# Gated embedding added by transfers, and a ninth pair by seven products, in the last stage of a Hymba block

## The chip, the cores and the metric

The kernel runs on one core of a Trainium2 chip. The metric is the device time of one execution in microseconds (us), taken as the median of several runs. A core has TensorE (PE in the profile, with PEld for its weight loads), VectorE (DVE), ScalarE (ACT), GpSimd (POOL) and SyncE (SP), which run side by side and wait for each other on semaphores, and 16 DMA engines. DMAs are put on queues by SP, by ACT and by POOL.

## The reference

One layer of a block over 256 positions and 4096 columns. Its last part, which the change is in:

```python
h = h + jnp.concatenate([y_a, y_c], axis=-1) @ w_out[i]
gate = jax.nn.sigmoid(rms_norm(h, ple_norm_g[i]) @ w_ple_gate[i] + b_ple_gate[i])
h = h + gate * (p[i] @ w_ple[i])
return rms_norm(h, final_g)
```

`w_ple_gate` is 4096 x 4096, `w_ple` is 256 x 4096; all is float32.

## The kernel before

A matrix product of 256 positions by 4096 rows of weights is made for two blocks of 512 columns at a time. That is a *group*; the last stage has four, and `c0` = 0, 2, 4, 6 is the first of each group's two blocks. I call them groups 1 to 4. The rows are walked in 16 *pairs* of two blocks of 128. `product` and `mixed_product` load a pair's weights (`wt`) with SP and split each into a rounded high part `wh`, cast by ACT (L204), and a low part `wl` = `wt` - `wh`, made by DVE (L205). Each product is made three times (high by high, low by high, high by low).

A *plain* pair takes 2 x 2 x 2 x 3 = 24 products of TensorE. A pair *by seven* uses Strassen's scheme in Winograd's form: 7 x 3 = 21, for which DVE sums weights into `ua` and `ub` (L518, L519, L531, L532), and these are split too, into `uh` and `ul`. It also needs combined left sides, which `combined_parts` makes ahead. For pair 13 there is no tile for them; `combine_into_places(13, ...)` puts them into free corners of the first four operand tiles, once for each left operand.

The string of pairs (`dense`, `denser`, `late`, `final`) is the order of a group. `*` is a pair by seven; `-` means that the low part of its second block is made by a transfer: ACT writes the negated high part into `low` (L217), and a DMA on POOL's queue adds the weights to it (L495, L524).

`later` is a queue of small work of the group before. `fill` takes four of its entries after each pair (`fills=(4,)`). In the last stage these are, for each of the four quarters (256 positions in two halves `h`, two blocks `j`): the gate times the embedding (`z`), the sum of that and the residual `hc`, the sum of squares of `hc` (ACT, L610) and `hc` times the last weight `fgs`. All but the squares are by DVE, and the profile has them at L184. The group's own end is the product of the embedding (`product(w_ple[0], ...)`, 24 products at L237).

The program gives the order in which the work is written; a scheduler then sets each engine's order by its own estimates of durations. Each engine takes its instructions in that order. Only what is in `pin` keeps the order in which it is written. Buffers of one `tag` go round: `wh` and `wl` have three each, `uh` and `ul` two.

Of the kernel before, what the change touches and what calls it, by code (L numbers as in the profile page):

```python
# [13 lines left out]
ALU = mybir.AluOpType  # L14
# [11 lines left out]
def hybrid_block(  # L26
# [23 lines left out]
    nc = tc.nc  # L50
# [129 lines left out]
    later = deque()  # L180
# [62 lines left out]
    def product(w, col, lhs, kblocks, pool=None, tag="acc", fills=2):  # L243

        acc = [
            (pool or ps_acc).tile([P, NB], F32, tag=tag, name=f"acc{h}") for h in range(NH)
        ]
        for k0 in range(0, kblocks, KC):
            kc = min(KC, kblocks - k0)
            wh, wl = weight_parts(w, col, k0, kc)  # L250
            for k in range(kc):
                for h in range(NH):
                    accumulate(acc[h], h, lhs, k0 + k, wh, wl, k, kblocks)
            fill(fills)
        return acc
# [10 lines left out]
    def sum_rows():  # L266
        return [spool.tile([P, NB], F32, tag="row", name="comb", bufs=3) for _ in range(2)]
# [33 lines left out]
    def combine_again(dst, at, t, i, rows, then=lambda ins: None, at_places=None):  # L301

        a, s = rows
        then(
            nc.vector.tensor_tensor(
                a.rearrange("q (i t) -> q i t", t=T), t[:, i : i + 2, 0, :].bitcast(F32),
                t[:, i : i + 2, 1, :].bitcast(F32), ALU.add,
            )
        )
        return combined_parts(  # L310
            dst, at, s, a[:, :T], a[:, T : T + P], a[:, T + P :], 1.0, then, at_places
        )
# [27 lines left out]
    def units(text):  # L340

        return [
            (int(u.rstrip("*+-")), "".join(f for f in "*+" if f in u), "-" in u)
            for u in text.split()
        ]


    dense = units("1 0* 3 2* 5 4* 6* 7 8* 9 10* 11 12* 14* 13 15")
    denser = units("1 0* 3 2* 5 4* 13* 7- 6*- 8* 10*- 9 12* 14* 11 15")
# [12 lines left out]
    late = units("1 3 5 7 9 11 13 15 0* 2 4* 6 8* 10* 12 14")  # L362

    def spare_places(tiles):

        return [[t[:, 0, q, P:] for q in range(2)] for t in tiles]
# [3 lines left out]
    def combine_into_places(pair, tiles):  # L370

        rows = sum_rows()
        places[pair] = spare_places(tiles[:4])
        t, i = tiles[pair // 2], pair % 2 * 2
        combine_again(None, None, t, i, rows, at_places=places[pair])()
# [193 lines left out]
    tt, stt = nc.vector.tensor_tensor, nc.vector.scalar_tensor_tensor  # L569
    QUARTERS = ((0, 0), (1, 0), (0, 1), (1, 1))  # L570

    def helper_sums(helper, z):


        nc.scalar.copy(z[1][0], helper["P1"])
        tt(z[1][0], helper["P6"], z[1][0], ALU.add)
        tt(z[0][1], helper["P5"], z[1][0], ALU.add)
        tt(z[1][0], helper["P7"], z[1][0], ALU.add)
        tt(z[1][1], helper["P5"], z[1][0], ALU.add)

    def sum_tiles(*homes):

        homes = homes or (dict(tag="stage"),) * 2
        t = [spool.tile([P, NH, NB], F32, name="z", **kw) for kw in homes]
        return t, [[t[j][:, h] for j in range(2)] for h in range(NH)]
# [481 lines left out]
    def broadcast_row(src, n0, n, **kw):  # L1067

        kw = kw or dict(tag="row", bufs=3)
        t = spool.tile([P, n], F32, name="row", **kw)  # L1070
        nc.sync.dma_start(
            t, bass.AP(tensor=src.tensor, offset=src.offset + n0, ap=[[0, P], [1, n]])
        )
        return t
# [101 lines left out]
    hs, hT, hS = [], [], []  # L1176
# [20 lines left out]
    for c0 in range(0, D // NB, 2):  # L1197
        for j in range(2):
            hc = act.tile([P, NH, NB], F32, tag="act", name="hc")
# [20 lines left out]
        for h, j in QUARTERS:  # L1220
            hc = hs[c0 + j][:, h, :]
# [10 lines left out]
    ssq_f = cpool.tile([P, NH, n_f + 2], F32, name="ssq_f")  # L1232
    nc.vector.memset(ssq_f[:, :, :1], EPS)
    square_f = partial(square_sum, scale=D ** -0.5)

    def gated_pair(c0, order, ahead):

        z, rows, fgs = [], [], []

        def on_begin():  # L1240
            rows.extend(broadcast_row(b_ple_gate, (c0 + j) * NB, NB) for j in range(2))

        def on_helpers(helper):
            z.extend(sum_tiles()[1])
            stt(z[0][0], helper["P1"], r_h[:, :1], rows[0], ALU.mult, ALU.add)
            helper_sums(helper, z)
            for h, j in QUARTERS[1:]:
                zz = z[h][j]
                stt(
                    zz, zz, r_h[:, h : h + 1], rows[j],  # L1250
                    ALU.mult, ALU.subtract if j else ALU.add,
                )
            fgs.extend(broadcast_row(final_g, (c0 + j) * NB, NB) for j in range(2))

        acc = mixed_product(
            w_ple_gate[0], c0 * NB, hT, hS, order, on_helpers, ahead=ahead, fills=(4,),
            on_begin=on_begin,
        )
        pacc = [
            product(w_ple[0], (c0 + j) * NB, pT, PLE // P, pool=ps_tmp, tag="tmp", fills=0)  # L1260
            for j in range(2)
        ]
        todo = []
        for h, j in QUARTERS:
            gt, hc = z[h][j], hs[c0 + j][:, h, :]
            stt(gt, acc[h][j], r_h[:, h : h + 1], gt, ALU.mult, ALU.subtract if j else ALU.add)
            nc.scalar.activation(gt, gt, AF.Sigmoid)
            later.append(partial(tt, gt, pacc[j][h], gt, ALU.mult))
            todo.append(partial(tt, hc, hc, gt, ALU.add))
            todo.append(partial(square_f, ssq_f[:, h, 1 + c0 + j : 2 + c0 + j], hc))  # L1270
            todo.append(partial(tt, hc, hc, fgs[j], ALU.mult))
        later.extend(todo)

    for c0 in range(0, n_f - 2, 2):
        gated_pair(c0, dense if c0 else late, None if c0 else h_ahead)


    c0 = n_f - 2
# [9 lines left out]
    rows, fgs = [], []  # L1288
# [90 lines left out]
    squares = []  # L1379
# [45 lines left out]
```

## Time and profile before

| | us |
|---|---|
| median of the runs | 2024.87 |
| lowest run | 2024.77 |
| profiled execution | 2025.85 |
| its span (first to last instruction) | 2024.1 |
| PE busy in it | 2006.7 |
| DVE busy | 1926.9 |
| ACT busy | 1257.1 |
| POOL busy | 65.3 |

Busy time counts stretches in which at least one instruction of an engine runs; matmuls overlap, and their ends are modelled, so a busy PE is not proof of PE at its peak. Start times are us from the span's start. In the chain of waits each row is what the end of the span was waiting for at that moment. In groups of instructions the first number after the bar is the busy time, the second the mean of one in ns, then the idle time of the engine just before and what ended it. The time "to landing" runs from a DMA's issue to the update of its semaphore.

### The profile page before, as it was taken

To read this page: it belongs to the slowest core of one execution; us is meant where nothing else is said; L and a number is where in the kernel's file an instruction comes from. 1 tells how busy PE (TensorE), PEld (TensorE's weight loads), DVE (VectorE), ACT (ScalarE), POOL (GpSimd) and SP (SyncE) were. 2 spreads that over 40 slices of the span, in tenths; PEclk is the share of its full clock that TensorE was granted. 3 is DMA by queue.
4 is the path that set the end of the run, shared out by engine and by line. 5 is a ranking of instruction groups with operands and counts; after the bars stand their busy time and mean duration, and the time that the engine had idled before them with its cause. 6 is when DMAs were issued, how large, how long until landed. Compare 5 with 4: busy or idle time off the path is not lost.

```text
span 2024.1 us, 26329 instructions
## 1 busy us (share of the span) xinstructions
PE 2006.7 (99%) x9043; PEld 1648.0 (81%) x9043; DVE 1926.9 (95%) x2771; ACT 1257.1 (62%) x1634; POOL 65.3 (3%) x71
## 2 busy tenths in 40 slices
PE   9999999999999999999999999999999999999997
PEld 7888888878888888788888888887888888888876
DVE  7999999899999999888999999999999999999998
ACT  7655555665666556776566676765766766656565
POOL 0000000000000000000000000000000000000000
PEclk9999999999999999999999999999999999999999
DMA  8788878679668877556677786876767766666765
GB/s 290 225 233 241 249 221 250 178 220 257 200 198 257 255 206 235 164 176 205 202 239 215 225 244 209 240 239 204 236 215 230 234 200 200 211 218 206 232 207 180
DMA packets 174193, 447.72 MB, mean 221 GB/s; under 512 B 14302, under 2 KB 17518, under 8 KB 174058
## 3 DMA queue, kind: packets, MB, share of 16 engines
q1 hardware_dynamic: 161952, 417.93, 63.8%
q0 software_dynamic: 11456, 27.27, 7.9%
q8 instruction: 71, 1.16, 0.2%
q10 hardware_dynamic: 650, 0.84, 0.1%
q14 instruction: 64, 0.52, 0.1%
HBM read 441.78 MB, written 4.19 MB: 220 GB/s over the span
## 4 chain that ended last, share of the span: by engine, by line
PE 89%; DVE 6%; issue 2%; DMA 1%; ACT 1%; POOLq 0%; POOL 0%; ACTq 0%; DVEq 0%; SPq 0%
PE acc L420 68%; PE acc_P L420 17%; DVE wl L205 2%; DMA wt<-in_w_in_dram 1%; PE tmp_ps L170 1%; DVE cv L787 1%; PE acc L237 1%; DVE ul L205 1%; PE tmp_ps L959 0%; PE tmp_ps L943 0%; PE tmp_ps L977 0%; ACT uh L204 0%; DVE cv L868 0%; ACT wh L204 0%; PE tmp_ps L982 0%
## 5 line engine op out<-in xcount | busy, mean ns | idle before, releaser
L420 PE MATMUL acc<-wh,big_t 128*128 128x512 f32 x4028 | 1240.3, 391 | 0.9 <-ACT big_t L156 0.4
L204 ACT CAST wh<-wt 128x1024 fp32r<-128x1024 f32 (+1 forms) x716 | 684.3, 965 | 493.8 <-PE acc L420 351.7
L420 PEld LDWEIGHTS acc<-wh,big_t 128*128 128x128 f32 x4028 | 753.3, 188 | 157.1 <-issue 1.3
L205 DVE TENSOR_TENSOR wl<-wt,wh 128x1024 fp32r<-128x1024 f32 (+1 forms) x716 | 788.8, 1113 | 33.0 <-ACT wh L204 27.5
L420 PE MATMUL acc<-wl,big_t 128*128 128x512 f32 x1958 | 756.4, 392 | 0.3 <-DVE wl L205 0.2
L420 PEld LDWEIGHTS acc<-wl,big_t 128*128 128x128 f32 x1958 | 367.2, 188 | 78.1 <-DVE wl L205 2.7
L204 ACT CAST uh<-ua 128x1024 fp32r<-128x1024 f32 x187 | 196.6, 1051 | 103.0 <-DVE ua L519 51.7
L205 DVE TENSOR_TENSOR ul<-ua,uh 128x1024 fp32r<-128x1024 f32 x187 | 228.1, 1220 | 6.9 <-ACT uh L204 4.2
L787 DVE SCALAR_TENSOR_TENSOR cv<-uT,dw,cv 128x255 f32<-128x255 f32 (+23 forms) x480 | 203.6, 463 | 1.1
L420 PE MATMUL acc_P<-uh,big_t 128*128 128x512 f32 x570 | 174.6, 391 | 0.1
L204 ACT CAST uh<-ub 128x1024 fp32r<-128x1024 f32 x99 | 104.2, 1053 | 47.9 <-DVE ub L532 39.2
L420 PEld LDWEIGHTS acc_P<-uh,big_t 128*128 128x128 f32 x570 | 106.0, 188 | 24.5 <-ACT uh L204 3.3
L205 DVE TENSOR_TENSOR ul<-ub,uh 128x1024 fp32r<-128x1024 f32 x99 | 120.8, 1220 | 0.8 <-ACT uh L204 0.5
L420 PE MATMUL acc_P<-ul,big_t 128*128 128x512 f32 x285 | 109.7, 392 | 0.2 <-DVE ul L205 0.2
L420 PE MATMUL acc<-uh,big_t 128*128 128x512 f32 x286 | 88.6, 390 | 0.0
L420 PE MATMUL acc_P<-wh,big_t 128*128 128x512 f32 x286 | 88.3, 389 | 0.0
L518 DVE TENSOR_TENSOR ua<-wt 128x512 f32<-128x512 f32 x112 | 76.9, 686 | 10.0 <-DMA wt<-in_w_in_dram 6.2
L519 DVE TENSOR_TENSOR ua<-wt 128x512 f32<-128x512 f32 x112 | 76.8, 686 | 2.7 <-DMA wt<-in_w_in_dram 1.7
L420 PE MATMUL acc_P<-uh,comb_t 128*128 128x512 f32 x228 | 70.3, 391 | 0.3 <-ACT uh L204 0.2
L532 DVE TENSOR_TENSOR ub<-ub,wt 128x512 f32<-128x512 f32 x99 | 68.1, 688 | 1.4
L531 DVE TENSOR_TENSOR ub<-ua,wt 128x512 f32<-128x512 f32 x99 | 67.8, 685 | 0.0
L420 PEld LDWEIGHTS acc_P<-ul,big_t 128*128 128x128 f32 x285 | 53.3, 188 | 13.9 <-DVE ul L205 3.0
(254 smaller groups left out, 1631.0 us busy)
## 6 DMA issues: line engine op xcount, KB each, us to landing
wt<-in_w_in_dram SPq DMA_DIRECT2D x416, 512.0 KB, 4.7
wt<-in_w_out_dram SPq DMA_DIRECT2D x128, 512.0 KB, 4.5
wt<-in_w_ple_gate_dram SPq DMA_DIRECT2D x128, 512.0 KB, 4.2
wt<-in_w_pw_dram SPq DMA_DIRECT2D x32, 512.0 KB, 4.9
ua<-in_w_in_dram SPq DMA_DIRECT2D x31, 512.0 KB, 4.3
ua<-in_w_in_dram POOLq DMA_DIRECT2D x31, 512.0 KB, 8.8
wt<-in_w_in_dram SPq DMA_DIRECT2D x31, 256.0 KB, 2.8
low<-in_w_in_dram POOLq DMA_DIRECT2D x12, 512.0 KB, 8.2
```

Of the source, the lines that this page charges most:

```text
L170: nc.tensor.transpose(pt[:, i * T + h * P : i * T + (h + 1) * P], src[:, h, b] if len(src.shape) == 4 else src[:, h, b * P : (b + 1) * P], ...
L204: nc.scalar.copy(wh[:, :kc, :], wt[:, :kc, :]),
L205: nc.vector.tensor_tensor(wl[:, :kc, :], wt[:, :kc, :], wh[:, :kc, :].bitcast(F32), ALU.subtract),
L237: nc.tensor.matmul(acc, a, b[:, k, :], start=kb == 0 and kind == 0, stop=kb == kblocks - 1 and kind == 2,)
L420: nc.tensor.matmul(banks[name], a, b, start=name not in begun, stop=final and ends[name] == n and kind == 2 and not (left and name in "P2 ...
L518: plus(ua[:, 0], w0[:, 0], w0[:, 1])
L519: plus(ua[:, 1], w0[:, 1], w1[:, 1])
L531: plus(ub[:, 0], ua[:, 0], w1[:, 1])
L532: plus(ub[:, 1], ub[:, 0], w1[:, 0])
L787: nc.vector.scalar_tensor_tensor(cv[:, i, PAD - k :], uT[:, i, : T + k - PAD], dw[:, b, k : k + 1], cv[:, i, PAD - k :], ALU.mult, ALU.add,)
```

## The change

It has three parts.

- The sum of gated embedding and residual (`tt(hc, hc, gt, ALU.add)` on DVE, twelve in all) becomes a DMA on POOL's queue that adds `gt` to `hc`. It is written right behind the product that makes `gt`. Squares and weighted copies are written after all four of them, squares first.
- Groups 2 and 3 use `denser` in place of `dense`: nine pairs by seven in place of eight, and three low parts by transfers in place of none.
- `combine_into_places(13, hT)` is called once, after group 1.

```diff
-        todo = []
+        squares, weights = [], []
         for h, j in QUARTERS:
             gt, hc = z[h][j], hs[c0 + j][:, h, :]
             stt(gt, acc[h][j], r_h[:, h : h + 1], gt, ALU.mult, ALU.subtract if j else ALU.add)
             nc.scalar.activation(gt, gt, AF.Sigmoid)
             later.append(partial(tt, gt, pacc[j][h], gt, ALU.mult))
-            todo.append(partial(tt, hc, hc, gt, ALU.add))
-            todo.append(partial(square_f, ssq_f[:, h, 1 + c0 + j : 2 + c0 + j], hc))
-            todo.append(partial(tt, hc, hc, fgs[j], ALU.mult))
-        later.extend(todo)
+            later.append(partial(nc.gpsimd.dma_start, hc, gt, accum_op=ALU.add))
+            squares.append(partial(square_f, ssq_f[:, h, 1 + c0 + j : 2 + c0 + j], hc))
+            weights.append(partial(tt, hc, hc, fgs[j], ALU.mult))
+        later.extend(squares + weights)
 
     for c0 in range(0, n_f - 2, 2):
-        gated_pair(c0, dense if c0 else late, None if c0 else h_ahead)
+        gated_pair(c0, denser if c0 else late, None if c0 else h_ahead)
+        if c0 == 0:
+            combine_into_places(13, hT)
```

The two orders and the functions that the new call uses (unchanged):

```python
    dense = units("1 0* 3 2* 5 4* 6* 7 8* 9 10* 11 12* 14* 13 15")
    denser = units("1 0* 3 2* 5 4* 13* 7- 6*- 8* 10*- 9 12* 14* 11 15")
...
    def combine_into_places(pair, tiles):

        rows = sum_rows()
        places[pair] = spare_places(tiles[:4])
        t, i = tiles[pair // 2], pair % 2 * 2
        combine_again(None, None, t, i, rows, at_places=places[pair])()
```

ACT's order at the start of group 2, before (`junk` with `ssq_f` is a square of `hc`; what stands in brackets are the semaphores waited for, DMASW those of POOL's DMAs, DMAHW those of SP's, DVE, PE and Activation those of the engines):

```order
L204 CAST uh<-ua 128x1024 [waits DVE_49]
L204 CAST wh<-wt 128x1024 [waits DMAHW4_49,PE_49,Activation_49]
L204 CAST wh<-wt 128x1024 [waits DMAHW5_49,DVE_49,PE_49]
L204 CAST wh<-wt 128x1024 [waits DMAHW6_49,DVE_49,PE_49]
L204 CAST uh<-ub 128x1024 [waits DVE_49]
L610 ACTIVATE junk,ssq_f<-hc 128x512
L204 CAST wh<-wt 128x512 [waits DMAHW7_49,PE_49,Activation_49]
L610 ACTIVATE junk,ssq_f<-hc 128x512 [waits DVE_49,Activation_49]
```

The same place now:

```order
L204 CAST uh<-ua 128x1024 [waits DVE_49]
L610 ACTIVATE junk,ssq_f<-hc 128x512 [waits DMASW4_49]
L610 ACTIVATE junk,ssq_f<-hc 128x512 [waits DMASW5_49,Activation_49]
L204 CAST wh<-wt 128x1024 [waits DMAHW3_49,PE_49]
L204 CAST uh<-ub 128x1024 [waits DVE_49]
L204 CAST wh<-wt 128x1024 [waits DMAHW4_49,PE_49]
L204 CAST wh<-wt 128x1024 [waits DMAHW5_49,PE_49]
L610 ACTIVATE junk,ssq_f<-hc 128x512 [waits DMASW6_49,Activation_49]
L204 CAST wh<-wt 128x512 [waits DMAHW6_49,DVE_49,PE_49]
L610 ACTIVATE junk,ssq_f<-hc 128x512 [waits DMASW7_49,Activation_49]
```

The squares have moved ahead of the cast `wh` and of `uh<-ub`, and each now waits for a DMA of POOL's queue.

DVE's order at the same place, before (`z<-acc` is the product with the embedding, `hc<-hc,z` the sum):

```order
L205 TENSOR_TENSOR ul<-ua,uh 128x1024 [waits Activation_49]
L205 TENSOR_TENSOR wl<-wt,wh 128x1024 [waits PE_49,Activation_49]
L531 TENSOR_TENSOR ub<-ua,wt 128x512
L184 TENSOR_TENSOR hc<-hc,z 128x512
L532 TENSOR_TENSOR ub<-ub,wt 128x512 [waits DVE_49]
L184 TENSOR_TENSOR hc<-hc,z 128x512
L205 TENSOR_TENSOR wl<-wt,wh 128x1024 [waits DMAHW5_49,PE_49,Activation_49]
L205 TENSOR_TENSOR ul<-ub,uh 128x1024 [waits Activation_49]
```

The same place now:

```order
L205 TENSOR_TENSOR ul<-ua,uh 128x1024 [waits Activation_49]
L532 TENSOR_TENSOR ub<-ub,wt 128x512 [waits DVE_49]
L205 TENSOR_TENSOR wl<-wt,wh 128x1024 [waits PE_49,Activation_49]
L184 TENSOR_TENSOR z<-acc_15625,z 128x512
L205 TENSOR_TENSOR ul<-ub,uh 128x1024 [waits Activation_49]
L184 TENSOR_TENSOR z<-acc_15626,z 128x512
L205 TENSOR_TENSOR wl<-wt,wh 128x1024 [waits DMAHW4_49,PE_49,Activation_49]
L205 TENSOR_TENSOR wl<-wt,wh 128x1024 [waits DMAHW5_49,PE_49,Activation_49]
L205 TENSOR_TENSOR wl<-wt,wh 128x512 [waits DMAHW6_49,PE_49,Activation_49]
```

The sums are gone, and the third and fourth products have moved behind the `wl` and `ul` that need ACT's casts.

ACT's order at the start of group 3, before:

```order
L204 CAST uh<-ua 128x1024 [waits DVE_49]
L204 CAST wh<-wt 128x1024 [waits DMAHW3_49,PE_49,Activation_49]
L204 CAST wh<-wt 128x1024 [waits DMAHW4_49,PE_49,Activation_49]
L204 CAST uh<-ub 128x1024 [waits DVE_49]
L610 ACTIVATE junk,ssq_f<-hc 128x512 [waits DVE_49]
```

The same place now:

```order
L204 CAST uh<-ua 128x1024 [waits DVE_49]
L610 ACTIVATE junk,ssq_f<-hc 128x512 [waits DMASW3_49]
L610 ACTIVATE junk,ssq_f<-hc 128x512 [waits DMASW4_49,Activation_49]
L204 CAST wh<-wt 128x1024 [waits DMAHW3_49,PE_49]
L204 CAST wh<-wt 128x1024 [waits DMAHW4_49,PE_49]
L204 CAST uh<-ub 128x1024 [waits DVE_49]
```

Two squares now come ahead of three casts, where one stood behind them.

## The prediction

> **What bounds the kernel now.** I read the page first, then the chain of waits, then the stage by windows.
>
> ```profile
> span 2024.1 us, 26329 instructions
> PE 2006.7 (99%) x9043; PEld 1648.0 (81%) x9043; DVE 1926.9 (95%) x2771; ACT 1257.1 (62%) x1634; POOL 65.3 (3%) x71
> ```
>
> TensorE is the bound, VectorE (DVE) is close behind, and ScalarE (ACT) and GpSimd (POOL) have room. The chain of waits in the last stage (start, length, what; x is a count) shows how close:
>
> ```profile
> 1740.13 5.44 PE acc L237 x24
> ...
> 1747.01 1.14 issue
> 1748.15 1.06 ACT wh L204
> 1749.23 1.23 DVE wl L205
> ...
> 1780.50 1.06 ACT uh L204
> 1781.60 0.73 PE acc_P L420 x2
> ...
> 1827.88 5.44 PE acc L237 x24
> ...
> 1915.73 5.44 PE acc L237 x24
> ```
>
> The rows of 24 are the embedding products that end groups 1, 2 and 3, so group 2 runs from 1745.57 to 1833.32 and group 3 to 1921.17. They also give the pitch of a product: 5.44 / 24 = 0.227 us. Between 1747 and 1781.6 the chain leaves PE and runs through DVE and ACT: in the first third of group 2 every microsecond that DVE loses is one that PE loses.
>
> ```profile
> 1745.57:1833.32 87.75, 87.70 (x386) 71.56 (x385) 87.02 (x106) 52.42 (x64) 0.00 (x0) 1.00 0.67 217
> 1833.32:1921.17 87.85, 87.85 (x385) 71.64 (x385) 86.98 (x107) 51.92 (x64) 0.00 (x0) 1.00 0.69 215
> ```
>
> The windows (columns: length, PE, PEld, DVE, ACT, POOL busy, clock, DMA share, GB/s) have DVE busy for 87.0 of 87.8 us. A group has 8 plain pairs of 24 products, 8 sevens of 21 and 24 of the embedding: 384 x 0.2267 = 87.05 us. So PE loses 0.7 and 0.8 us in these groups; the clock is full.
>
> **The change, part by part.** Durations, from the groups of instructions (mean ns after the busy time):
>
> ```profile
> L184 DVE TENSOR_TENSOR hc<-hc,z 128x512 f32<-128x512 f32 x12 | 8.1, 685 | 0.0
> L205 DVE TENSOR_TENSOR wl<-wt,wh 128x1024 fp32r<-128x1024 f32 x573 | 693.4, 1219 | 32.7 <-ACT wh L204 27.4 <-ACT qT L986 2.3 <-PE tmp_ps L170 1.5
> L205 DVE TENSOR_TENSOR wl<-wt,wh 128x512 fp32r<-128x512 f32 x143 | 98.0, 685 | 0.3 <-ACT wh L204 0.2
> L518 DVE TENSOR_TENSOR ua<-wt 128x512 f32<-128x512 f32 x112 | 76.9, 686 | 10.0 <-DMA wt<-in_w_in_dram 6.2 <-DMA wt<-in_w_out_dram 2.7 <-DMA wt<-in_w_ple_gate_dram 1.0
> L217 ACT ACTIVATE low<-wh 128x1024 fp32r<-128x1024 f32 x21 | 22.3, 1062 | 0.6
> L305 DVE TENSOR_TENSOR comb<-big_t 128x512 f32<-128x512 f32 x18 | 12.4, 686 | 0.1
> L276 DVE TENSOR_TENSOR comb<-comb 128x128 f32<-128x128 f32 x33 | 9.4, 286 | 0.9 <-ACT comb L298 0.7
> L610 ACT ACTIVATE junk<-hc 128x512 bf16<-128x512 f32 x31 | 19.5, 628 | 3.9 <-DVE hc L1332 2.3 <-DVE hc L1222 1.3
> L610 ACT ACTIVATION_READ_ACCUMULATOR junk<-hc 128x1 f32 x33 | 6.2, 187 | 0.0
> L524 POOL DMA_DIRECT2D low<-in_w_out_dram x6 | 5.2, 864 | 37.2 <-ACT low L217 25.9 <-PE acc_P L420 11.3
> ```
>
> 1. *Ninth seven.* Three products fewer in groups 2 and 3: 2 x 3 x 0.2267 = -1.36 us of PE. On DVE a seven takes four sums (4 x 0.686), one short low part (0.685) and three long ones (3 x 1.219): 7.1 us against 2.4 for a plain pair, so +4.6 us.
> 2. *Three low parts by transfers.* DVE -3 x 1.219 = -3.7 us a group, ACT +3 x 1.062 in a queue that is 60% busy, POOL three issues of 0.86 on an idle queue. They come from the eighth pair on, behind the tight third. With 1, DVE +1.0 us a group. I cost the ACT part at nothing: its cover is 35 us of idle ACT a group; without it each row would cost its 1.06.
> 3. *Places for pair 13.* Once: DVE 0.686 + 8 x 0.286 = 3.0 us, nearly all of it in the first third of group 2, where it takes the room of the adds taken out.
> 4. *Twelve adds off DVE.* -4 x 0.685 = -2.7 us at the starts of groups 2, 3 and 4. Net of 1 to 4, DVE: group 2 +1.2, group 3 -1.8, group 4 -2.7. Group 3's loss of 0.8 us should go, and as much in group 4: -1.6 us.
> 5. *Twelve transfers that add `z` into `hc`.* POOL's issues are free. Queued behind them on POOL are the low parts, 30 us later. What costs is the new wait: ACT's squares of `hc` now wait for a landing, and they have moved ahead of the casts (`wh`, `uh`) that DVE and PE need. ACT works in order, so a late landing holds the casts.
>
> No row shows a transfer from `z` into `hc`; the nearest are these (KB each, median us from issue to landing; then the spread for `low`):
>
> ```profile
> wt<-in_w_in_dram SPq DMA_DIRECT2D x416, 512.0 KB, 4.7
> ...
> wt<-in_w_in_dram SPq DMA_DIRECT2D x31, 256.0 KB, 2.8
> low<-in_w_in_dram POOLq DMA_DIRECT2D x12, 512.0 KB, 8.2
> ```
>
> ```profile
> DMA to landing us min/median/max: 5.8/8.3/10.0
> ```
>
> Plain transfers of half the size land in 2.8 / 4.7 = 0.6 of the time. The adding ones scaled so: 3.5, 4.9, 6.0 us. I take 4.9, the median, because the DMA share here (0.67) is ordinary. The second of a pair issues 0.86 us later and shares the queue; I let it land 1.9 us (4.7 - 2.8) after the first, at 6.8; the fast end is 3.5 and 4.4, the slow end 6.0 and 7.9.
>
> [...]
>
> *Group 2, by hand*, from the timeline:
>
> ```profile
> 1743.34 1.28 DVE L184 TENSOR_TENSOR z<-acc,z 128x512 f32<-128x512 f32 x2
> 1749.23 1.23 DVE L205 TENSOR_TENSOR wl<-wt,wh 128x1024 fp32r<-128x1024 f32 x1
> 1752.79 1.22 DVE L205 TENSOR_TENSOR wl<-wt,wh 128x1024 fp32r<-128x1024 f32 x1
> 1753.92 1.22 DVE L205 TENSOR_TENSOR ul<-ub,uh 128x1024 fp32r<-128x1024 f32 x1
> 1755.61 0.39 PE L420 MATMUL acc_P<-ul,big_t 128*128 128x512 f32 x1
> ```
>
> The first product is done near 1744.3 (0.3 later than now, for one moved row of 3). Landings at 1749.2 and 1751.1; the second square ends 0.8 later (0.628 + 0.187), the cast behind it 1.06 after that, at 1752.95. DVE reaches the `wl` that needs this cast at about 1749.6 (1749.23 now): 3.3 us idle. The third product follows at 1754.7; its transfer lands at 1759.6, its square ends at 1760.4, the short cast at 1761.05. DVE by then has a `ul`, a product and two `wl` done (1.13, 0.60, 1.13, 1.13: 1753.92 - 1752.79, and the second of two in 1.28) and has waited since 1758.75: 2.3 us. PE had `ul` 0.47 us ahead (1755.61 - 1755.14) and about 0.3 later: 3.3 + 2.3 - 0.4 = 5.2 us. Fast end 1.5, slow end 7.5.
>
> *Groups 3 and 4*: with no places and four adds fewer, only the first pair of landings binds, through the cast `uh<-ub`:
>
> ```profile
> 1831.54 1.22 DVE L205 TENSOR_TENSOR wl<-wt,wh 128x1024 fp32r<-128x1024 f32 x1
> 1838.61 2.00 ACT L204 CAST wh<-wt 128x1024 fp32r<-128x1024 f32 x2 [0.76 <-ACT uh L204]
> 1842.00 0.62 PE L420 MATMUL acc_P<-uh,big_t 128*128 128x512 f32 x2
> 1919.66 1.23 DVE L205 TENSOR_TENSOR wl<-wt,wh 128x1024 fp32r<-128x1024 f32 x1
> 1930.01 0.62 PE L420 MATMUL acc_P<-uh,big_t 128*128 128x512 f32 x2
> ```
>
> Group 3: the product now stands behind this `wl`, done at 1833.4; second landing 1840.2, square 1841.0, two `wh` and `uh` 3.0 more: 1844.0 against a use at 1842.0, 2.0 us late (0.4 to 3.1). Group 4: product 1921.5, landing 1928.3, square, one `wh`, `uh`: 1931.1 against 1930.0, 1.1 us late (0 to 2.3).
>
> Sum: -1.4 - 1.6 + 5.2 + 2.0 + 1.1 = +5.3 us. The profiled execution took 2025.85 us with its span of 2024.1; the median of the runs is 2024.87, so the forecast is 2030 us. The ends: waits of 1.9 and 12.9 give 2023.8 and 2034.8.
>
> **Rivals.** *The landings are early enough (faster by a little).* If the second square is over before DVE asks for its cast, nothing is lost and PE keeps -1.36 - 1.6: 2021.9 us. Place: the two squares in front of the casts at each group's start. The whole change turns from loss to gain when the waits sum to 3.0 us, near a first landing of 3.8 us. For it: 3.5 is the scaled minimum, and the source is on the chip; against it, no adding transfer so far landed under 5.8 for twice the size. [...]
>
> *DVE alone decides.* Landings are hidden, but group 2's extra 1.2 us of DVE does not fit in 87.75 us: -1.36 - 1.6 + 1.2 + 0.7 (the loss by balance) gives 2023.8. For it: DVE's 87.02 busy; against it: the transfers spare DVE after the eighth pair.
>
> *The landings are late.* 6.0 us or more, with queueing behind weight loads: 2035 and above.
>
> **How the numbers follow.** Forecast 0.57 (2024 to 2035), gain 0.24, DVE alone 0.09, late 0.10. The likeliest case gives 2030. The range 2021.5 to 2035 leaves out about half of the late case and a third of the gain: under 0.2. All cases lie within 2% (40 us), about what a measurement here can tell from no change: same 0.98, 0.01 each for faster and slower.
>
> **What would show it.** Right: squares of `hc` on ACT with several us of idle before them, released by the transfer; a DVE gap behind `wh` near 1750; PE gaps of some 5 us in group 2, less in 3 and 4; groups of 381 x 0.2267 = 86.4 us plus these. Wrong: landings under 3.5 us, no gap before the squares, groups near 86.4, or a loss in the second half of a group, where the low parts are.

## The result, and the profile after

The changed kernel takes 2043.32 us (median of 6 runs, 2038.95 to 2047.55) against 2025.85 for the kernel before on the same chip. The ratio is 1.0086, with a 95% interval of 1.0073 to 1.0099: slower by 0.9%, where 2030 had been forecast with a range of 2021.5 to 2035. One of the six runs of the kernel before took 4118.48 us, for a reason that no trace here shows; the medians of that kernel beside the experiments below, 2025.65 to 2026.42, bear out the 2025.85. The profiled execution took 2047.55 us and is the slowest of the six, so the stages below show somewhat more loss than the median has. Its page, the span and the busy time of each engine:

```profile
span 2045.8 us, 26375 instructions
PE 2012.9 (98%) x9037; PEld 1650.0 (81%) x9037; DVE 1924.7 (94%) x2774; ACT 1266.5 (62%) x1648; POOL 81.2 (4%) x89
```

TensorE makes six products fewer (x9037 against x9043) and yet is busy 6.2 us longer. That is the first thing to explain: work that is the same or less, and takes more time. The windows of groups 2, 3 and 4 of the changed kernel, the last one up to 2028.37 (length, busy time of PE, PEld, DVE, ACT and POOL, granted clock, DMA share, GB/s), and behind them group 4 of the kernel before, up to the same place:

```profile
1748.51:1842.61 94.10, 88.80 (x383) 70.60 (x382) 86.43 (x112) 57.35 (x73) 5.03 (x6) 1.00 0.77 231
1842.61:1938.69 96.08, 90.61 (x382) 73.25 (x382) 86.08 (x107) 56.68 (x69) 6.15 (x7) 0.96 0.75 225
1938.69:2028.37 89.68, 87.01 (x371) 69.68 (x371) 82.78 (x104) 51.11 (x64) 4.49 (x5) 0.98 0.62 191
```

```profile
1921.17:2007.21 86.04, 85.86 (x372) 68.16 (x371) 84.15 (x107) 50.42 (x64) 0.93 (x1) 1.00 0.58 184
```

Group 2 grew from 87.75 to 94.10 us, group 3 from 87.85 to 96.08, and from the start of group 4 to the end of the span it is 107.11 (2045.8 - 1938.69) against 102.93. That is 6.35 + 8.23 + 4.18 = 18.8 us of the 21.7 between the spans. The other 2.9 us were there before group 2 began (1748.51 against 1745.57), in code that is the same in both; in the profiles of the experiments below, whose code ahead of group 2 is also the same, that start lies anywhere between 1744.0 and 1748.3. I count them to neither side. Note the clock: 0.96 in group 3 and 0.98 in group 4, where it was full before. It is not this execution alone: over the whole span the six runs of the change have 0.993 to 0.996, and those of before beside the experiments 0.997 or 0.998.

The chain of waits of the changed kernel at the starts of groups 2 and 3 (start, length, what):

```profile
1747.95 5.94 DMA hc<-z
...
1754.70 0.94 ACT wh L204
...
1755.67 1.01 DVE wl L205
...
1759.88 6.11 DMA hc<-z
...
1766.80 0.95 ACT uh L204
...
1843.06 0.60 POOL hc L184
1843.66 7.39 DMA hc<-z
...
1851.85 1.88 ACT wh L204 x2
1853.73 0.96 ACT uh L204
...
1890.61 8.11 DMA low<-in_w_ple_gate_dram
```

Where the chain of before ran through DVE and ACT, it now begins with a transfer, then a cast. ACT's timeline at the start of group 3 shows how (in brackets: idle time before, and what ended it):

```profile
1846.10 1.05 ACT L204 CAST uh<-ua 128x1024 fp32r<-128x1024 f32 x1
1848.61 0.63 ACT L610 ACTIVATE junk<-hc 128x512 bf16<-128x512 f32 x1 [1.46 <-DMA hc<-z]
1849.14 0.19 ACT L610 ACTIVATION_READ_ACCUMULATOR junk<-hc 128x1 f32 x1
1851.13 0.63 ACT L610 ACTIVATE junk<-hc 128x512 bf16<-128x512 f32 x1 [1.80 <-DMA hc<-z]
1851.67 0.18 ACT L610 ACTIVATION_READ_ACCUMULATOR junk<-hc 128x1 f32 x1
1851.76 1.97 ACT L204 CAST wh<-wt 128x1024 fp32r<-128x1024 f32 x2
1853.64 1.04 ACT L204 CAST uh<-ub 128x1024 fp32r<-128x1024 f32 x1
```

`wh` and `uh<-ub` read nothing that the squares make; what ties them together is their place in the queue. PE's timeline at the same place:

```profile
1851.06 0.39 PE L420 MATMUL acc<-wl,big_t 128*128 128x512 f32 x1
1854.73 0.73 PE L420 MATMUL acc_P<-uh,big_t 128*128 128x512 f32 x2 [3.29 <-ACT uh L204]
...
1857.06 0.63 PE L420 MATMUL acc<-wh,big_t 128*128 128x512 f32 x1
1857.49 0.63 PE L420 MATMUL acc_P<-ul,big_t 128*128 128x512 f32 x1
1857.91 0.63 PE L420 MATMUL acc<-ul,big_t 128*128 128x512 f32 x1
```

PE stands until `uh` is there, 3.44 us beyond its pitch (1854.73 - 1851.06 - 0.227). Then products begin 0.427 us apart (1857.49 - 1857.06), not 0.227: eight of them, 1.6 us more. The windows of that stretch, cut at the edges of the slow one:

```profile
1848.92:1852.33 3.41, 2.52 (x12) 1.75 (x10) 1.47 (x3) 1.61 (x5) 1.78 (x2) 1.00 0.78 241
1852.33:1855.75 3.42, 1.02 (x4) 0.86 (x5) 2.26 (x2) 3.42 (x6) 0.00 (x0) 1.00 1.01 179
1855.75:1859.16 3.41, 3.41 (x9) 2.63 (x8) 3.41 (x6) 0.80 (x3) 0.00 (x0) 0.50 0.55 180
1859.16:1862.57 3.41, 3.41 (x16) 2.81 (x15) 1.28 (x2) 2.01 (x2) 0.00 (x0) 1.00 0.75 240
```

The granted clock is 0.50 for 3.41 us, behind a stretch of the same length in which PE was busy for 1.02 us only. This happens three times: in group 3 here and behind a second wait, and in group 4. That second wait, again in PE's timeline:

```profile
1896.18 0.39 PE L420 MATMUL acc<-wl,big_t 128*128 128x512 f32 x1
1898.76 0.50 PE L420 MATMUL acc<-low,big_t 128*128 128x512 f32 x1 [2.19 <-DMA low<-in_w_ple_gate_dram]
```

No square is in this wait: a low part that a transfer makes lands at 1898.72 (1890.61 + 8.11 in the chain above). PE stands 2.35 us for it (1898.76 - 1896.18 - 0.227), and seven products at half clock follow.

### The profile page after: what moved, and what is told of

Same layout as the page of the kernel before. It is cut to its first block, busy times and chain, and to the rows that moved or that the text cites. A ratio compares the mean times of both kernels' runs of the same rounds, so it can differ in the third digit from the quotient of the medians.

```text
span 2045.8 us, 26375 instructions
## 1 busy us (share of the span) xinstructions
PE 2012.9 (98%) x9037; PEld 1650.0 (81%) x9037; DVE 1924.7 (94%) x2774; ACT 1266.5 (62%) x1648; POOL 81.2 (4%) x89
## 5 line engine op out<-in xcount | busy, mean ns | idle before, releaser
L204 ACT CAST wh<-wt 128x1024 fp32r<-128x1024 f32 (+1 forms) x710 | 676.8, 963 | 480.5 <-PE acc L420 352.3
L205 DVE TENSOR_TENSOR wl<-wt,wh 128x1024 fp32r<-128x1024 f32 (+1 forms) x710 | 779.9, 1109 | 47.6 <-ACT wh L204 42.3
L420 PE MATMUL acc<-wl,big_t 128*128 128x512 f32 x1930 | 748.5, 392 | 0.8 <-DVE wl L205 0.8
L420 PEld LDWEIGHTS acc<-wl,big_t 128*128 128x128 f32 x1930 | 362.5, 188 | 78.0 <-DVE wl L205 3.0
L420 PE MATMUL acc_P<-uh,big_t 128*128 128x512 f32 x582 | 179.3, 392 | 8.3 <-ACT uh L204 6.1
```

The lines of the kernel that those rows point to most:

```text
L204: nc.scalar.copy(wh[:, :kc, :], wt[:, :kc, :]),
L205: nc.vector.tensor_tensor(wl[:, :kc, :], wt[:, :kc, :], wh[:, :kc, :].bitcast(F32), ALU.subtract),
L420: nc.tensor.matmul(banks[name], a, b, start=name not in begun, stop=final and ends[name] == n and kind == 2 and not (left and name in "P2 ...
```

## The experiments

My theory after this (T1): ACT's squares wait for landings in front of casts, DVE and PE starve behind them, and PE's idle time lowers the clock. Its rivals are two: the ninth seven and the places overload DVE (T2); the adding transfers delay other transfers by their traffic (T3). The times in one table, each against the runs of before that were made with it:

| kernel | median us | before | ratio, 95% interval |
|---|---|---|---|
| the change | 2043.32 | 2025.85 | 1.0086 [1.0073, 1.0099] |
| order only | 2034.19 | 2025.74 | 1.0037 [1.0024, 1.0051] |
| transfers only | 2048.70 | 2025.74 | 1.0112 [1.0097, 1.0127] |
| change, squares later | 2024.75 | 2025.74 | 0.9998 [0.9989, 1.0008] |
| change, sums on POOL itself | 2039.43 | 2025.74 | 1.0072 [1.0055, 1.0089] |
| change, sums back on DVE | 2030.37 | 2026.42 | 1.0018 [1.0009, 1.0027] |
| change, squares and low parts later | 2024.72 | 2026.42 | 0.9990 [0.9981, 0.9999] |
| change, with zero products | 2046.44 | 2026.42 | 1.0096 [1.0081, 1.0112] |
| transfers only, squares later | 2023.76 | 2026.42 | 0.9987 [0.9978, 0.9996] |
| before, with made gaps | 2046.53 | 2025.65 | 1.0102 [1.0073, 1.0131] |
| change, low parts later | 2042.57 | 2026.00 | 1.0086 [1.0070, 1.0103] |

**The two halves apart.** First the ninth seven, the low parts and the places, with the sums on DVE where they were (from the change):

```diff
-        squares, weights = [], []
+        todo = []
...
-            later.append(partial(nc.gpsimd.dma_start, hc, gt, accum_op=ALU.add))
-            squares.append(partial(square_f, ssq_f[:, h, 1 + c0 + j : 2 + c0 + j], hc))
-            weights.append(partial(tt, hc, hc, fgs[j], ALU.mult))
-        later.extend(squares + weights)
+            todo.append(partial(tt, hc, hc, gt, ALU.add))
+            todo.append(partial(square_f, ssq_f[:, h, 1 + c0 + j : 2 + c0 + j], hc))
+            todo.append(partial(tt, hc, hc, fgs[j], ALU.mult))
+        later.extend(todo)
```

> Keeps the ninth seven, the three low parts by transfers and the places of pair 13 in groups 2 and 3; the sums of hc and z go back to DVE at their old place, so no square waits for a landing. T1 (the squares wait for landings in front of the casts, and that is what costs): the loss is gone, -1.4 us of products and up to +2 us of DVE in group 2: 2023 to 2027 us beside a before of 2025, no square idle for a transfer, no PE gap above 2 us at the starts of groups 2, 3 and 4, hence no products at half clock there. T2 (the ninth seven and the places overload DVE): the loss stays, 2037 to 2045. A part of its own: the low part that came late in group 3 (PE waits near 1896 to 1899 in the profile after, about 2.4 us and 1.4 us of slower products behind it). If the low transfers alone cause it, that gap stays here and the time is 2028 to 2030; if the adding transfers and the late group start cause it, it is gone.

Measured 2034.19: between the two theories. No square waits and no row of products runs at half clock, but groups 2 and 3 are longer than before:

```profile
1748.33:1837.54 89.21, 88.50 (x382) 70.55 (x382) 88.56 (x115) 57.63 (x73) 2.67 (x3) 1.00 0.76 232
1837.54:1927.48 89.94, 88.57 (x383) 70.56 (x382) 88.17 (x110) 56.93 (x69) 2.61 (x3) 1.00 0.75 228
```

DVE is busy for 88.56 and 88.17 us, more than the 86.4 us that PE needs for 381 products. So T2 fits this half by itself: with the sums still on DVE, the nine sevens leave DVE no room. The late low part hardly shows here: PE waits for one once, for 0.5 us.

Then the adding transfers alone:

```diff
-        gated_pair(c0, denser if c0 else late, None if c0 else h_ahead)
-        if c0 == 0:
-            combine_into_places(13, hT)
+        gated_pair(c0, dense if c0 else late, None if c0 else h_ahead)
```

> Keeps the twelve adding transfers and the squares in front of the casts; groups 2 and 3 go back to eight sevens without low parts by transfers, and pair 13 is combined where it was. T1: the squares still idle some 16 us for transfers, PE still has gaps of 2.5 us and more at the starts of the three groups: 2035 to 2041 us, that is +10 to +16 beside a before of 2025 (the change's loss less the late low part of group 3). T2 (the ninth seven and the places overload DVE): within 3 us of before, or faster.

Measured 2048.70, more than the whole change and outside what T1 had for it. The idle time of ACT before the squares, first in this kernel, then in the change:

```profile
  DMA hc<-z: 30.3, 12
```

```profile
  DMA hc<-z: 16.1, 8
```

All twelve squares wait here, and eight in the change. So the transfers cost 23 us alone and the order 8.5 alone, and both together 17.5: the second half hides part of the first. The four squares of the change that do not wait are the second pairs of groups 3 and 4. In group 3 the two transfers of that pair are issued 0.6 us apart in the change (1850.19 and 1850.79) and 3.2 apart here (1850.66 and 1853.90), and ACT stands 4.03 us before the last square here.

**The squares moved.** They are queued on ACT behind casts of the next pairs; the first two of each group, the ones with casts waiting behind them, come 9 to 13 us later, counted from the group's start:

```diff
-        later.extend(squares + weights)
+        def behind(square):
+            with queued_behind(recent):
+                square()
+
+        idle_turns = [lambda: None] * 4
+        later.extend(idle_turns + [partial(behind, s) for s in squares] + weights)
```

> The whole change, with one move: the squares of hc are queued on ACT some 9 us later, behind casts of the next pairs, so that their transfers have landed when ACT reaches them. T1: the idle time of ACT before the squares falls from 16 us to under 2, the PE gaps at the starts of the three groups go and with them the products at half clock: 2021 to 2027 us. T2: no change against the change itself, 2037 to 2045. T3 (the adding transfers delay weight loads and low parts by their traffic): stays at +8 us or more over before, with the waits moved to tiles that transfers fill.

Measured 2024.75. No square waits for a transfer any more, no product of the three groups runs at half clock, and the loss is gone; for the loss as a whole T2 and T3 fall. The windows of groups 2 and 3:

```profile
1744.79:1833.33 88.54, 87.14 (x382) 71.12 (x382) 86.42 (x112) 57.63 (x73) 5.01 (x6) 1.00 0.82 246
1833.33:1920.60 87.27, 87.27 (x382) 70.94 (x382) 85.96 (x107) 56.26 (x69) 6.12 (x7) 1.00 0.82 246
```
The same move with the transfers alone (`dense`, without the places):

> The adding transfers alone, without the ninth seven, the places and the low parts, and with the squares queued some 9 us later. Beside the transfers with the squares in front (2048.7 us) this differs by the squares' place alone. If the waits behind the squares are all of the loss: ACT's idle time before the squares falls from 30 us to under 2 and the time to that of before or a little less, 2022 to 2027 us. If the transfers cost by their traffic or their issue: 2030 and above, with PE waiting for weight loads.

Measured 2023.76, against 2048.70 with the squares in front: 25 us for the place of twelve instructions of 0.63 us on an engine that is 62% busy. Nothing else is rewritten in either pair of kernels; with the squares, the weighted copies of `hc` come at another place, and the scheduler puts some neighbours in another order. The transfers land no sooner (DMA issues of groups 2 and 3, KB each, median us to landing; first with the squares in front, then with them later):

```profile
hc<-z POOLq DMA_DIRECT2D x8, 256.0 KB, 6.1
```

```profile
hc<-z POOLq DMA_DIRECT2D x8, 256.0 KB, 6.2
```

The landing by itself is not the cost; what stands behind the wait is. This version is faster than before, by 0.13% (0.04 to 0.22%), and than the change.

**The sums by another engine.** POOL makes each sum itself:

```diff
-            later.append(partial(nc.gpsimd.dma_start, hc, gt, accum_op=ALU.add))
+            later.append(partial(nc.gpsimd.tensor_tensor, hc, hc, gt, ALU.add))
```

> The whole change, but the sums are made by GpSimd itself in place of a transfer that it issues, at the same places and with the squares still in front of the casts. No row shows such a sum on GpSimd; bounded by DVE's 0.69 us below and the transfers' 4 to 7 us above. T1: the loss follows the time from issue to the sum's end: at 1 to 2 us for one the squares wait little, 2021 to 2028 us; at 4 us or more nothing is gained, 2037 and above. T2: 2037 to 2045 whatever the sum takes. T3 (traffic): the traffic is gone, so at or below before even where a sum takes 3 us.

Measured 2039.43. A sum takes 1.29 to 2.27 us on POOL, and T1 then wanted 2028 at most: a miss. Ten squares still wait for POOL, 10.1 us in all, so T1 has a part in this loss, and its size was not separated. DVE's and POOL's timelines at the start of group 3 show what was overlooked:

```profile
1837.12 1.41 DVE L205 TENSOR_TENSOR wl<-wt,wh 128x512 fp32r<-128x512 f32 x1
1838.45 1.78 DVE L518 TENSOR_TENSOR ua<-wt 128x512 f32<-128x512 f32 x1
1840.15 0.68 DVE L519 TENSOR_TENSOR ua<-wt 128x512 f32<-128x512 f32 x1
```

```profile
1836.69 2.99 POOL L184 TENSOR_TENSOR hc<-hc,z 128x512 f32<-128x512 f32 x2 [37.85 <-DVE z L184]
```

While POOL adds, DVE's instructions of 0.685 us take 1.41 and 1.78. In groups 2 to 4, up to the last embedding product, DVE is busy for 265.4 us in this kernel (89.77 + 89.50 + 86.15), 10.1 more than in the change (255.3), for twelve sums that would cost DVE 8.2 (12 x 0.685). A low part was late here too (PE stands 2.59 us behind 1887.80).

On DVE, at the new place and with the squares in front:

```diff
-            later.append(partial(nc.gpsimd.dma_start, hc, gt, accum_op=ALU.add))
+            later.append(partial(tt, hc, hc, gt, ALU.add))
```

> The whole change with its new order, squares of hc in front of the casts, but each sum of hc and z is made by DVE (0.69 us) at the transfer's place. If the wait for the landings is what costs: no square waits more than about 1 us and the time is that of the kernel with the order only, 2032 to 2036 us. If the place of the squares in front of the casts costs by itself (0.8 us of ACT each): 2037 and above. If DVE alone decided, moving the sums back should add DVE's 12 x 0.69 = 8.2 us to the change: 2048 and above.

Measured 2030.37, under even the lowest expectation, and 3.8 us under the order only. So squares in front of casts show no cost of their own where their sum comes soon; and moving DVE's 8.2 us back made the change some 13 us faster, which T2 cannot give.

**The late low part.** In groups 2 and 3 the products with such a part stand a pair later, first with the squares later, then in the change as it is (the other line with `waiting.append` likewise; `low_turns` is 2 there, 1 elsewhere):

```diff
-                    waiting.append((n + 1, partial(add_plain, n, 1, wh, low, kinds=(2,))))
+                    waiting.append((n + low_turns, partial(add_plain, n, 1, wh, low, kinds=(2,))))
```

> The change with the squares queued later, and in groups 2 and 3 the products with a low part brought by a transfer one pair later (some 16 products, 3.6 us). In the kernel with the squares later PE still waits 1.8 us for such a low part in group 2 (1793.2 to 1795.0). If the low part is late because PE asks one pair after its issue, that wait goes and nothing else changes: 1.5 to 2 us less than with the squares later alone, 2022 to 2024 us. If the low parts follow PE (their tile or their issue waits for PE's progress), the wait moves with the product and the time stays.

> The change as it is, squares in front of the casts, but the products with a low part brought by a transfer stand one pair (some 16 products, 3.6 us) later in groups 2 and 3. In the change PE waits 2.2 us for such a low part in group 3 (until 1898.76) and seven products behind that wait run at half clock (1.4 us). If the late low part is a loss of its own: 3 to 4 us less than the change, 2037 to 2041 us, and no PE wait for low. If it only stands in front of another shortage (as with the squares later, where a wait of 1.6 us for a cast took its place): the wait moves to a cast or a weight load and the time stays at 2041 to 2046.

Measured 2024.72 and 2042.57, against 2024.75 and 2043.32 without this edit: no gain in either. The wait moved. In the second, PE stands 2.32 us behind 1893.11, now for a `uh` whose cast stands behind this one on ACT:

```profile
1893.62 1.04 ACT L204 CAST wh<-wt 128x1024 fp32r<-128x1024 f32 x1 [2.51 <-PE acc L420]
```

The releaser named there was done long before; the weights of this cast were issued at 1885.87 and landed at 1893.52, 7.65 us later. Time to landing of the weight loads in groups 2 and 3, first before, then in the change:

```profile
DMA to landing us min/median/max: 3.4/4.2/5.2
```

```profile
DMA to landing us min/median/max: 3.4/4.6/8.3
```

And the DMA share in the stretch of group 3 with the low parts, in the change:

```profile
1877.00:1899.00 22.00, 19.81 (x87) 15.78 (x86) 21.93 (x27) 17.32 (x19) 2.61 (x3) 1.00 0.89 258
```

The low parts and the weight loads take time of the same 16 DMA engines (POOL's queue 15.9% of it in groups 2 and 3, SP's 59.8%), which are 0.89 busy here, and DVE is busy for 21.93 of the 22 us. Where the products with the low part stand later, the next weight load is what comes late. T3 fits at this place, with the low parts as most of the traffic: the slowest weight load of groups 2 and 3 takes 8.5 us in the order only, 6.9 in the transfers only and 5.2 before. No run takes the low parts alone out of the change.

**The clock.** Ten products by a tile of zeros in front of the waiting product of each group, to keep PE at work (without the lines that make the tile and set `warm_at` to 1):

```diff
+            if n == warm_at:
+                for _ in range(10):
+                    made.append(
+                        nc.tensor.matmul(
+                            banks["P5"], zero, lhs[0][:, 0:2, 0, :], start=False, stop=False
+                        )
+                    )
             add("P6", s_of(2), (ubh[:, 0], ubl[:, 0]), n, True)
```

> The change, with ten products by a tile of zeros (10 x 0.227 = 2.3 us, they add nothing to the sums) on PE in front of the product that waits in the first seven of groups 2, 3 and 4; the planner shifts some rows of DVE and ACT with them. If PE's idle time of 2.5 us and more is what halves the clock: no product at 0.427 us behind them, the gaps fall under 1.5 us, and groups 3 and 4 lose 1.6 us less each: 2037 to 2043 us. If the half clock follows from anything else (power, the waits of other engines), eight products at 0.427 us still follow, and the time stays at 2043 or grows by up to 2.3 us a group.

Measured 2046.44, and inconclusive: the scheduler counts the zero products as work and put products that wait ahead of them, so the starts of two products still lie 2.3 to 3.2 us apart at each place. The other way round decides it: waits made on PE in the kernel before, where nothing else waits (the edit shortened; `zero_product` is a product by a tile of zeros).

```diff
+            if n in stalls:
+                zero_product()
+                nc.gpsimd.dma_start(zero, zero_from)
+                stall.append(stalls[n])
...
+                    if stall and stall[0] == 0:
+                        zero_product()
```

> The kernel before, unchanged in its work, with five waits made on PE in the middle of groups 2, 3 and 4: a product by a tile of zeros, a 64 KB transfer into that tile that POOL issues behind it, and a second product by the tile that waits for the landing; 1, 3, 5, 7 and 9 products of the kernel stand between the two, so PE's idle time shrinks by 0.45 us from one to the next, from some 3 us (a landing of 2 to 3 us, estimated from the 2.0 to 2.9 us of the output transfers, and POOL's issue) to some 1. Nothing waits on ACT or DVE here and no transfer adds into hc. If PE's idle time by itself halves the clock: six to eight products at 0.427 us behind the gaps of 2.2 us and more (1.2 to 1.6 us lost each), none behind the gaps under 2; time about 10 us above before. If the half clock in the change comes from something else that the waits go with (ACT, the adding transfers): no product at 0.427 us behind any of the five.

Measured 2046.53, 21 us above before where about 10 were expected, from two runs. The gaps did not come in the planned sizes: PE stands for 2.8 to 3.2 us in four and 1.4 in one, as later landings took longer (the waiting product starts 2.89 us behind POOL's issue at the first gap, 3.67 at the third). Of the four, three have half-clock products behind them (eight, seven and five), one has none, and the short one has none. Windows of 3.41 us again, at the first gap and at the one without:

```profile
1768.93:1772.34 3.41, 2.27 (x10) 1.52 (x9) 3.41 (x5) 1.57 (x2) 0.60 (x1) 1.00 0.89 312
1772.34:1775.76 3.42, 1.52 (x7) 1.26 (x8) 3.42 (x6) 1.74 (x2) 0.00 (x0) 1.00 0.72 219
1775.76:1779.17 3.41, 3.41 (x10) 2.65 (x9) 3.41 (x5) 1.40 (x2) 0.00 (x0) 0.50 0.55 186
...
1867.92:1871.33 3.41, 2.14 (x10) 1.43 (x8) 3.41 (x5) 2.56 (x4) 0.53 (x1) 1.00 0.91 301
1871.33:1874.74 3.41, 1.78 (x8) 1.49 (x9) 3.41 (x5) 0.88 (x1) 0.00 (x0) 1.00 0.60 184
1874.74:1878.16 3.42, 3.42 (x16) 2.66 (x15) 1.59 (x3) 2.52 (x3) 0.00 (x0) 1.00 0.51 153
```

So half-clock products stood here behind PE's waits with no square, cast or adding transfer into `hc` in play. The length of a wait alone does not decide: the first gap, of 3.2 us, has slow products behind it, and the one of 3.1 us at 1872.96 has none. The window with 1.52 us of PE work was followed by a slow one; those with 1.78 us and more were not.

## Why the prediction was wrong, step by step

The direction and the mechanism of step 5 were right: squares with idle time in front, released by the transfer, a DVE gap, and PE gaps in all three groups. Its sizes and two things costed at nothing were not. The step that failed is the price of the waits in step 5. The forecast was -3.0 us for steps 1 and 4 and +8.3 for the waits (5.2 + 2.0 + 1.1). By the experiments the change without the squares in front of the casts is 1.0 us faster than before (2024.75 against 2025.74), and putting them there costs 18.6 (2043.32 against 2024.75). The profiled execution shows where. Measured against the forecast for the same stretch:

- *Group 2*: 87.75 - 0.68 + 5.2 = 92.3 forecast, 94.1 measured. The term of 5.2 was 1.8 too small, in its range (to 7.5).
- *Group 3*: 87.85 - 0.68 - 0.8 + 2.0 = 88.4 against 96.1. The wait of 2.0 measured 3.44; 2.35 is the late low part, 1.6 and 1.4 the clock; some 0.9 are smaller gaps.
- *Group 4 to the end*: 102.93 - 0.8 + 1.1 = 103.2 against 107.1. The wait of 1.1 measured 2.3 (1949.73 - 1947.19 - 0.227) and had a second of 0.7 behind it; 1.6 is the clock.

These misses sum to 1.8 + 7.7 + 3.9 = 13.4 us: 4.6 of clock, 2.35 of the late low part, 6.4 of waits that were sized too small and of smaller gaps beside them.

*The landings* were a small part of the error: 4.9 for the first of a pair was taken, and 6.8 for the second, both from the first's issue. They were 4.2, 5.5 and 5.2, and 6.6, 8.0 and 7.9 for the first pairs of groups 2, 3 and 4, and over all twelve transfers, each from its own issue:

```profile
DMA to landing us min/median/max: 4.0/5.1/7.4
```

The second ones of groups 3 and 4 lay at the slow end (7.9 had been given for it), and the first transfer of group 3 is issued 0.45 us behind the start of the group (1843.06 against 1842.61) where 0.1 was used, that of group 4 0.45 where 0.3 was. These are the 1.2 to 1.4 us by which groups 3 and 4 wait longer.

*The clock* is the term that was missing altogether. The prediction read 1.00 in the windows of before and carried it over. In the profiled execution three waits of PE, of 3.44, 2.35 and 2.3 us, have products at half clock behind them, and that is 4.6 us.

*Step 2, the low parts at nothing.* The cover named was idle ACT and an idle POOL queue. Both were idle. What came late was the transfer, on DMA engines that were 0.89 busy, and the row that spoke for it was quoted: 8.2 us to landing for `low`, against products that come one pair later.

*Steps 1 and 4, -1.36 and -1.6 us.* With the squares later, the transfers alone reach -0.13%, some 2.7 us, so taking the adds off DVE is worth about what step 4 said, or more. The ninth seven on top shows no gain: 0.9998 and 0.9990 with it, 0.9987 without, intervals overlapping. Against its 1.36 us of products stands a wait of PE in group 2: 1.56 us for a low part with the squares later, 1.40 for a `uh` with the low parts later too. That these waits are what eats the gain was not tested.

*Rivals.* "The landings are early enough" fell: 4.0 us was the fastest. "DVE alone" holds for the order without the transfers and not for the change. "The landings are late" has the measured time in its range, and mostly by luck: the median landing was 5.1 us where it asked for 6.0, late second landings give 2.6 of the 13.4 us, and the rest is what the waits held up and the clock. Its chance of 0.10, with the range cut at 2035, was too low: a chain of waits that each had a slow end was summed without asking what a longer wait brings with it.

## What to carry to other kernels

Before a transfer replaces a sum, look at what stands behind its reader on the reader's engine. Put the reader behind other work by at least the landing time, here 7 to 13 us later for the squares that hurt, and the same change turns from +17 us to none. When a forecast contains waits of PE of some us, ask for the clock: in the change three of 2.3 to 3.44 us had 3.41 us at half clock behind them, 1.4 to 1.6 us lost each, and two of 2.40 and 2.05 us had none. And count a new transfer against the DMA engines' share in its own stretch (0.89 where the late low part was), not against the idle engine that issues it.

## What the runs showed of the hardware

- *The half clock.* In the change products run at half clock three times in groups 2 to 4, for 3.41 us each. The spells begin at 1855.74, 1900.11 and 1951.31, which lie 44.37 and 51.20 us apart: 13.0 and 15.0 times 3.413. In windows of that length laid through them over the three groups, PE is busy for 1.02, 1.35 and 1.05 us in those just before the spells, and for 1.97 us or more in all others, and none of these has a slow one behind it. Two waits of PE in group 2, of 2.40 us (until 1757.55) and 2.05 (until 1774.94), fall into such windows. The windows of the made gaps fit: 1.52 us of PE work before a slow one, 1.78 and more before the others. By groups, the granted clock was 0.96, 0.98 and 0.98 in the transfers only and 1.00, 0.98 and 1.00 with the sums on POOL.
- *The product behind a wait.* In the change the product behind the wait of 3.44 us is followed 0.34 us later, not 0.227 (1855.07 behind 1854.73). It is the same after a wait of 0.21 us in the kernel before (1781.94 behind 1781.60): some 0.1 us at each of these.
- *POOL against DVE.* In the run with the sums on POOL, two of DVE's instructions on two tiles took 1.41 and 1.78 us beside such a sum, 2.1 and 2.6 times their 0.685. The pair of products `z<-acc`, whose one source is an accumulator of PE, took 1.28 us there (from 1835.92) with POOL's sum beside its last 0.5 us (from 1836.69), as it did in the kernel before without one (1.28 us from 1743.34).
